# A transformer trunk on one core: the last down projection with the activations as the stationary operand, and a final norm per partition

## The chip, the cores and the metric

The kernel runs on one core of one Trainium2 chip. The metric is the device time of one execution in microseconds (us); a kernel's time is the median of its runs.

## The reference, cut to what matters

A trunk of two layers over 256 tokens of 2048 features, all in fp32. What the change touches is the end of the second layer: the gated MLP, the residual sum and the final norm.

```
def conv_ffn(h, w_up, conv_w, conv_b, w_down):
    up = h @ w_up
    g, val = up[..., :D_FF], up[..., D_FF:]
    g = causal_dwconv(g, conv_w, conv_b)
    return (jax.nn.gelu(g) * val) @ w_down          # D_FF = 5632
...
        h = h + mix
        h = h + conv_ffn(rmsnorm(h, norm_ffn[layer]), ff_w_up[layer], ff_conv_w[layer],
                         ff_conv_b[layer], ff_w_down[layer])
    return rmsnorm(h, norm_final)                   # over the 2048 features of each token
```

## The kernel before

Activations lie feature-major: a tile has 128 features on the partitions and the 256 tokens along the free axis. The residual stream is `h[0..15]`, sixteen such tiles in eight SBUF tensors (lines 307 and 308). A factor of a matmul is held as a pair of float32r parts whose sum is exact: `split` (lines 271 to 280) makes [hi | lo] of an activation, 128x512, in a slot of the pool `s2k` (61 slots), and `convert` (lines 185 to 200) makes `hi` (ScalarE, line 198) and `lo` (VectorE, line 199) of a weight unit. All weights come as one stream of units of 128x1024 (512 KB), loaded by SP (line 175) four ahead and converted two ahead of the unit in use (`next_unit`, lines 202 to 210); `raw` has four buffers, `hi` and `lo` three each.

There are two matmul loops. `wstat` (lines 237 to 248) holds a weight tile stationary: for each 128x128 tile one matmul of hi with the 512 columns [xh | xl] and one of lo with the 256 columns xh. Its output is feature-major, in one of four PSUM buffers `acc`, as two halves that are added afterwards. `astat` (lines 250 to 263) holds the activations stationary: for each k tile and each half t of the tokens three matmuls, xh with hi, xh with lo and xl with hi, over cw weight columns, into one PSUM buffer for each t. Its output has 128 tokens on the partitions. It needs weights in the layout of `mov_stream` (lines 51 to 55) in place of `stat_stream` (lines 37 to 48). It is used with cw of 416 and 512 for z and v of layer 0, and with 512 for the v projection of layer 1 (lines 865 to 871).

Small work is woven into the loops: generators in the list `bg` are advanced a step by `tick()`, which `wstat` calls behind every second k tile and `astat` behind every k and t.

The last stage is `ffn(xs, sq, 1, "nfin", last=True)` at line 967. It makes the 44 tiles `act` (lines 791 to 804) and then calls `residual` (lines 752 to 779): for each of 16 output tiles m a `wstat` of 44 k tiles, two VectorE adds into `h[m]` (lines 770 and 771), a ScalarE product with the norm weight into `nxt` (line 775), and the square of `h[m]` summed on POOL (`Sq.add`, lines 328 to 342), the last one on VectorE. After that comes the final norm (lines 970 to 980): `sq.finish` (lines 354 to 367) sums over the partitions with matmuls against ones, makes the reciprocal root by eleven small VectorE instructions (`rv` at line 360, then `newton`), spreads it over the partitions with four more matmuls and copies it to `R`; then eight tiles are scaled by VectorE and POOL and stored from the queues of SP and ACT.

The instructions of each engine run in the order that the tile framework gives them, mostly that of the program; `pin` keeps an instruction in program order.

Of the kernel before, what the change touches and what calls it, by code (L numbers as in the profile page):

```python
# [36 lines left out]
def stat_stream(w, cols=None, front=0):  # L37
    """[K, N] -> units [U, 128, 1024]: eight 128x128 tiles each, k fastest;
    of the first `front` column tiles the last two k tiles come after the rest."""
    if cols is not None:  # L40
        w = w[:, cols]
    k, n = w.shape
    t = w.reshape(k // P, P, n // P, P).transpose(2, 0, 1, 3)
    if front:
        a = t[:front]
        t = np.concatenate([a[:, :-2].reshape(-1, P, P), a[:, -2:].reshape(-1, P, P), t[front:].reshape(-1, P, P)])
    t = t.reshape(-1, 8, P, P)
    return np.ascontiguousarray(t.transpose(0, 2, 1, 3)).reshape(-1, P, 1024)


def mov_stream(w, cw):
    """[K, N] -> units [U, 128, 2*cw]: two k tiles of a chunk of cw columns each."""
    k, n = w.shape
    t = w.reshape(k // 256, 2, P, n // cw, cw).transpose(3, 0, 2, 1, 4)
    return np.ascontiguousarray(t).reshape(-1, P, 2 * cw)
# [45 lines left out]
@with_exitstack  # L101
def trunk(ctx: ExitStack, tc: tile.TileContext, a, out):
# [17 lines left out]
    def slot(dt=F32):  # L120
        return sp.tile([P, 512], dt, tag="s2k", name=nm("s"))
# [23 lines left out]
    seq = []  # L145

    def add(name):
        ap = a[name]
        for u in range(ap.shape[0]):
            seq.append((ap, u, ap.shape[2]))  # L150
# [16 lines left out]
    def load():  # L167
        """one DMA of weights; the first ones bring the input along."""
        i = st["load"]
        if i >= len(seq):  # L170
            return
        st["load"] += 1
        ap, u, wd = seq[i]
        raw = wp.tile([P, 1024], F32, tag="raw", name=nm("raw"), bufs=4)[:, :wd]
        nc.sync.dma_start(out=raw, in_=ap[u])
        raws.append(raw)
        if i == 0:
            nc.sync.dma_start(out=vec[:, :KD], in_=a["vec"][:, :KD])
        if i < KD // 2:
            nc.sync.dma_start(out=h2[i], in_=a["x0"][i])  # L180
        if i == KD // 2:
            nc.sync.dma_start(out=con, in_=a["con"])
            nc.sync.dma_start(out=vec[:, KD:], in_=a["vec"][:, KD:])

    def convert():
        """weights as a pair of float32r parts whose sum is exact."""
        i = st["conv"]
        if i >= len(seq):
            return
        st["conv"] += 1  # L190
        raw, wd = raws[i], seq[i][2]
        raws[i] = None
        hi = wp.tile([P, 1024], F32R, tag="hi", name=nm("hi"))
        lo = wp.tile([P, 1024], F32R, tag="lo", name=nm("lo"))
        n = 2 if i < 2 else 1
        for c in range(n):
            q = slice(c * wd // n, (c + 1) * wd // n)
            A.copy(out=hi[:, q], in_=raw[:, q])  # L198
            V.tensor_tensor(lo[:, q], raw[:, q], hi[:, q].bitcast(F32), op=ALU.subtract)  # L199
        ready.append((hi, lo))  # L200
# [49 lines left out]
    def astat(kt, xs, cw):  # L250
        pst = [acc(), acc()]
        for k in range(kt):
            if k % 2 == 0:
                hi, lo = next_unit()
            o = (k % 2) * cw
            for t in range(2):
# [14 lines left out]
    def split(src, scale=None, dst=None):  # L271
        """[128,256] fp32 (SBUF or PSUM), times a per-partition scale -> [hi | lo]."""
# [9 lines left out]
    def newton(y, v, t):  # L282
        """y = v ** -0.5"""
# [37 lines left out]
    class Sq:  # L321
        """sum of squares over feature tiles; the last tile goes its own way."""
# [5 lines left out]
        def add(self, src, last=False, join=True):  # L328
# [3 lines left out]
            if last:  # L332
                if join:
                    eng.tensor_tensor(self.acc, self.acc, q, op=ALU.add)
                else:
                    self.parts.append(q)
# [32 lines left out]
        def spread(self, n):  # L369
            """the factor for feature-major tiles alone, on every partition."""  # L370
# [9 lines left out]
    def pending(sq, n=D, wait=6, hold=None):  # L380
        """the RMS factor, made a few steps into the next matmuls."""
# [12 lines left out]
    class Lazy(list):  # L394
        """entries are made when the matmul loop first reaches them."""
# [18 lines left out]
    # small tables that the layers read later  # L414
# [6 lines left out]
    def small_loads():  # L421
        pin(nc.gpsimd.dma_start(out=row, in_=a["row"].partition_broadcast(P)))
        yield
        for i in range(2):
            # spatial weights [j, g, i], block-lower-triangular part
# [38 lines left out]
    # ================= layer 0 mixer =================  # L464
# [6 lines left out]
    def gate_z(pst, c):  # L471
        """silu of a chunk of z; for chunk 0 the first 32 columns are dt."""
# [67 lines left out]
    def conv_tile(b, wname, n, width, taps, bias):  # L540
        """causal depthwise conv of a [128,256] tile along the free axis."""
# [122 lines left out]
    # gMLP, four chunks of 512 channels, the scan's groups woven in  # L664
# [50 lines left out]
    # gating by z, grouped RMS norm, back to feature-major  # L715
# [36 lines left out]
    def residual(kt, xin, wname, last=False, front=0):  # L752
        """front: that many tiles run ahead through all but the last two k tiles."""
# [8 lines left out]
        for m in range(KD):  # L762
# [9 lines left out]
            if last:  # L772
                if m % 2 == 0:
                    nxt.append(slot())
                A.activation(nxt[-1][:, (m % 2) * S:(m % 2 + 1) * S], h[m], AF.Identity, bias=0.0, scale=vc(wname, m))
            else:
                nxt.append(split(h[m], vc(wname, m)))
            sq.add(h[m], m == KD - 1, not last)
# [9 lines left out]
    def ffn(xs, sq, lay, wnext, last=False):  # L788
# [16 lines left out]
        return residual(KF, act, wnext, last)  # L805

    xs, sq = residual(32, Lazy(mix_in), "nf0")
    xs, sq = ffn(xs, sq, 0, "nm1")

    # ================= layer 1 mixer (MLA) =================  # L810
# [19 lines left out]
    def roped(x, o):  # L830
        """rotate the halves of two 64-row heads."""
# [80 lines left out]
    def step(kind, j):  # L912
        """one stage of the attention of heads 2j and 2j + 1."""
# [53 lines left out]
    hw, sq = ffn(xs, sq, 1, "nfin", last=True)  # L967

# [1 line left out]
    _, R, Rp = sq.finish(D)  # L970
    for q in range(KD // 2):
        if q == 0:
            for i in range(2):
                v = hw[q][:, i * S:(i + 1) * S]
                V.tensor_tensor(v, v, Rp, op=ALU.mult)
                (nc.scalar if i else nc.sync).dma_start(out=out[q][:, i * S:(i + 1) * S], in_=v)
            continue
        v = hw[q].rearrange("p (a b) -> p a b", a=2)
        (G if q in (3, 6) else V).tensor_tensor(v, v, R.unsqueeze(1).to_broadcast([P, 2, S]), op=ALU.mult)  # L979
        (nc.scalar if q % 2 else nc.sync).dma_start(out=out[q], in_=hw[q])  # L980
# [74 lines left out]
```

## Time and profile before

| | before |
|---|---|
| median of 3 runs | 2423.49 us |
| lowest and highest run | 2418.5 and 2424.66 us |
| span of the profiled execution | 2419.3 us (the page gives no other time of it) |
| mean granted TensorE clock | 0.995 |
| busy: TensorE, VectorE, ScalarE, POOL | 2386.0, 1582.7, 1189.3, 482.7 us |
| read from HBM, written to HBM | 431.15 MB, 2.10 MB |

A profile shows one execution. Engines are PE (TensorE matmuls), PEld (its weight loads), DVE (VectorE), ACT (ScalarE), POOL (GpSimd) and SP; "q" behind a name is that engine's queue. L133 is line 133, where all matmuls are issued, and L136 that of all transposes, so the names of the tiles tell them apart: `acc` is a projection, `ms` small work. Matmuls are pipelined: the duration of one is longer than the distance from its start to the next one's.

### The profile page before, as it was taken

The numbers are of one execution on the slowest core, as the hardware profiler recorded it, in microseconds if no ns is written. First come the engines' busy times: TensorE is split into PE (matmuls) and PEld (weight loads), VectorE is DVE, ScalarE is ACT, GpSimd is POOL, SyncE is SP. The second block draws the span as 40 slices with busy tenths as digits, with TensorE's granted clock in tenths as the row PEclk, the third lists the DMA queues.
The fourth block names the chain that finished last, engine by engine and source line by source line (L and its number), as shares of the span: only waits on it lengthen the run. The fifth ranks groups of instructions, "written<-read, shape, count | busy, mean of one in ns | idle before, by whom it ended". The sixth has DMA issues, their size and how long they took to land.

```text
span 2419.3 us, 35301 instructions
## 1 busy us (share of the span) xinstructions
PE 2386.0 (99%) x13479; PEld 2072.6 (86%) x13479; DVE 1582.7 (65%) x2371; ACT 1189.3 (49%) x1729; POOL 482.7 (20%) x452
## 2 busy tenths in 40 slices
PE   8999999999999999999999999999999999999997
PEld 6888888988888888888888887788888888888886
DVE  7677777665576666666555577778666666664544
ACT  5654444644455555555444445544555555554442
POOL 4111221022211112111111132123211111111111
PEclk9999999999999999999999999999999999999998
DMA  6565545666666666666666655356666666666664
GB/s 219 166 178 156 160 153 153 188 184 189 184 190 188 189 191 191 191 189 189 191 190 191 190 170 155 96 158 185 196 188 189 190 191 191 188 190 190 191 191 131
DMA packets 121913, 435.54 MB, mean 180 GB/s; under 512 B 13696, under 2 KB 14080, under 8 KB 121744
## 3 DMA queue, kind: packets, MB, share of 16 engines
q1 hardware_dynamic: 120672, 431.02, 59.3%
q8 instruction: 105, 1.72, 0.3%
q0 software_dynamic: 352, 1.10, 0.2%
q10 hardware_dynamic: 720, 1.18, 0.1%
q14 instruction: 64, 0.52, 0.1%
HBM read 431.15 MB, written 2.10 MB: 179 GB/s over the span
## 4 chain that ended last, share of the span: by engine, by line
PE 95%; DVE 2%; issue 1%; POOL 1%; ACT 1%; DMA 0%; SPq 0%; DVEq 0%; POOLq 0%; ACTq 0%
PE acc L133 91%; PE ms L133 4%; DVE lo L199 1%; PE ms L136 1%; DVE s L279 0%; ACT hi L198 0%; DMA raw<-in_z 0%; POOL t L550 0%; DVE t L545 0%; DVE s L979 0%; POOL s L818 0%; DVE s L276 0%; POOL t L331 0%; DVE s L634 0%; DVE t L268 0%
## 5 line engine op out<-in xcount | busy, mean ns | idle before, releaser
L133 PE MATMUL acc<-s,hi 128*128 128x512 f32 x5936 | 2072.9, 394 | 0.0
L133 PE MATMUL acc<-s,lo 128*128 128x256 f32 x5936 | 1656.4, 279 | 3.8 <-DVE lo L199 3.8
L199 DVE TENSOR_TENSOR lo<-raw,hi 128x1024 fp32r<-128x1024 f32 (+2 forms) x824 | 1015.9, 1233 | 700.1 <-ACT hi L198 693.9
L198 ACT CAST hi<-raw 128x1024 fp32r<-128x1024 f32 (+2 forms) x824 | 858.0, 1042 | 1088.3 <-PE acc L133 883.4
L133 PEld LDWEIGHTS acc<-s,hi 128*128 128x128 f32 x5936 | 1112.4, 187 | 255.6 <-issue 3.2
L133 PEld LDWEIGHTS acc<-s,lo 128*128 128x128 f32 x5936 | 1118.8, 188 | 5.6 <-DVE lo L199 4.8
L133 PE MATMUL acc<-hi,s 128*128 128x512 f32 (+1 forms) x640 | 198.6, 385 | 6.2 <-DVE s L279 5.7
L331 POOL TENSOR_TENSOR t<-h 128x256 f32<-128x256 f32 x60 | 66.9, 1114 | 588.1 <-DVE h L771 563.9
L801 POOL TENSOR_TENSOR t<-t,R 128x256 f32<-128x256 f32 x88 | 121.4, 1380 | 313.8 <-ACT t L800 309.9
L798 POOL TENSOR_TENSOR t<-t,R 128x256 f32<-128x256 f32 x88 | 68.9, 783 | 488.7 <-DVE t L268 453.4
L133 PEld LDWEIGHTS acc<-hi,s 128*128 128x128 f32 x640 | 121.4, 192 | 23.7 <-DVE s L279 8.4
L545 DVE SCALAR_TENSOR_TENSOR t<-t,vec,t 128x255 f32<-128x255 f32 (+2 forms) x248 | 120.7, 487 | 14.2 <-ACT t L543 9.7
L133 PE MATMUL acc<-lo,s 128*128 128x416 f32 (+1 forms) x320 | 121.8, 381 | 1.4 <-DVE lo L199 1.4
L268 DVE TENSOR_TENSOR t<-acc,t 128x256 f32<-128x256 f32 x233 | 97.4, 418 | 0.8 <-ACT t L267 0.8
L267 ACT COPY t<-acc 128x256 f32<-128x256 f32 x233 | 83.5, 359 | 0.3 <-PE acc L133 0.3
L133 PE MATMUL ms<-s,s 128*128 128x128 f32 (+4 forms) x424 | 78.2, 307 | 1.1 <-DVE s L930 0.6
L133 PEld LDWEIGHTS ms<-s,s 128*128 128x128 f32 (+1 forms) x424 | 60.1, 189 | 19.9 <-issue 9.0
L342 POOL TENSOR_TENSOR sqacc<-sqacc,t 128x256 f32<-128x256 f32 x60 | 72.8, 1213 | 4.7
L543 ACT ACTIVATE t<-t,vec 128x256 f32<-128x256 f32 x112 | 67.2, 600 | 12.9 <-POOL t L798 7.6
L133 PEld LDWEIGHTS acc<-lo,s 128*128 128x128 f32 x320 | 61.5, 192 | 8.4 <-DVE lo L199 2.1
L279 DVE SCALAR_TENSOR_TENSOR s<-h,vec,s 128x256 fp32r<-128x256 f32 x64 | 56.6, 895 | 1.0 <-ACT s L278 1.0
L803 DVE TENSOR_TENSOR t<-t,t 128x256 f32<-128x256 f32 x88 | 37.4, 426 | 28.6 <-POOL t L801 28.6
(174 smaller groups left out, 811.7 us busy)
## 6 DMA issues: line engine op xcount, KB each, us to landing
raw<-in_up SPq DMA_DIRECT2D x352, 512.0 KB, 4.2
raw<-in_down SPq DMA_DIRECT2D x176, 512.0 KB, 3.6
raw<-in_wout SPq DMA_DIRECT2D x64, 512.0 KB, 3.6
raw<-in_z SPq DMA_DIRECT2D x40, 416.0 KB, 3.6
raw<-in_x SPq DMA_DIRECT2D x32, 512.0 KB, 3.6
raw<-in_v SPq DMA_DIRECT2D x32, 512.0 KB, 3.7
raw<-in_u SPq DMA_DIRECT2D x32, 512.0 KB, 3.9
raw<-in_wo SPq DMA_DIRECT2D x32, 512.0 KB, 3.6
```

Of the source, the lines that this page charges most:

```text
L133: return nc.tensor.matmul(*args, **kw)
L198: A.copy(out=hi[:, q], in_=raw[:, q])
L199: V.tensor_tensor(lo[:, q], raw[:, q], hi[:, q].bitcast(F32), op=ALU.subtract)
L267: A.copy(out=b, in_=ps[:, S:])
L268: V.tensor_tensor(b, ps[:, :S], b, op=ALU.add)
L279: V.scalar_tensor_tensor(x[:, S:], src, scale, x[:, :S].bitcast(F32), op0=ALU.mult, op1=ALU.subtract)
L331: eng.tensor_tensor(q, src, src, op=ALU.mult)
L342: eng.tensor_tensor(self.acc, self.acc, q, op=ALU.add)
L543: A.activation(o, b, AF.Identity, bias=bias, scale=taps[width - 1])
L545: V.scalar_tensor_tensor(o[:, i:], b[:, :S - i], taps[width - 1 - i], o[:, i:], op0=ALU.mult, op1=ALU.add)
L798: G.tensor_tensor(b, b, R, op=ALU.mult)
L801: G.tensor_tensor(o, o, R, op=ALU.mult)
```

## The change

The last down projection goes from `wstat` to `astat`: four chunks of 512 output features, each with 44 k tiles and two halves of the tokens. The weights of that layer are laid out by `mov_stream`. The result has tokens on the partitions, so the residual is needed in that form too: a generator `by_token` transposes the sixteen tiles of `h` on TensorE, four to a PSUM buffer, and copies them to eight slots `ht[t][c]`; it runs in the ticks of the first chunk. It also loads the norm weights, broadcast over the partitions, from POOL's queue. Behind each chunk VectorE adds PSUM to `ht`, ScalarE squares the sum and adds the squares up along the free axis, and POOL multiplies by the norm weight (for half 0 of the last chunk VectorE does it, together with the factor). In the last unit of the last chunk the steps of half 0 come ahead of those of half 1 (`stagger`). The final factor is then one value per partition, made from `ss` by the same eleven small instructions. Eight tiles of 128x512 are scaled by VectorE and ScalarE and stored from the queues of SP, POOL and ACT. The matmuls against ones and those that spread the factor are gone for this norm. The host puts the output together for the new layout.

```
-    def astat(kt, xs, cw):
+    def astat(kt, xs, cw, stagger=False):
         pst = [acc(), acc()]
-        for k in range(kt):
-            if k % 2 == 0:
-                hi, lo = next_unit()
-            o = (k % 2) * cw
-            for t in range(2):
+        for u in range(kt // 2):
+            hi, lo = next_unit()
+            steps = [(k, t) for k in (2 * u, 2 * u + 1) for t in range(2)]
+            if stagger and u == kt // 2 - 1:
+                steps.sort(key=lambda q: q[1])
+            for k, t in steps:
+                o = (k % 2) * cw
                 xh = xs[k][:, t * P:(t + 1) * P]
...
-    hw, sq = ffn(xs, sq, 1, "nfin", last=True)
-
-    # ---- final norm ----
-    _, R, Rp = sq.finish(D)
-    for q in range(KD // 2):
...
+    act = ffn(xs, sq, 1)
+    ht = [[], []]
+    nw = []
+
+    def by_token():
+        for c in range(4):
+            nw.append(slot())
+            pin(nc.gpsimd.dma_start(out=nw[c], in_=a["nfin"][:, c * 512:(c + 1) * 512].partition_broadcast(P)))
+            for t in range(2):
+                ps = pmis()
+                for i in range(4):
+                    tr(ps[:, i * P:(i + 1) * P], h[4 * c + i][:, t * P:(t + 1) * P], ident)
+                yield
+                ht[t].append(slot())
+                A.copy(out=ht[t][c], in_=ps)
+                yield
+
+    bg.append(by_token())
+    ss = tiny([P, 4, 2], "fss", 1)
+    part_sum = tiny([P, 2], "fps", 1)
+    for c in range(4):
+        last = c == 3
+        pst = astat(KF, act, 512, last)
+        if c == 0:
+            flush()
+        for t in range(2):
+            o = ht[t][c]
+            V.tensor_tensor(o, pst[t], o, op=ALU.add)
+            jk = slot()
+            A.activation(jk, o, AF.Square, bias=0.0, scale=1.0, accum_out=ss[:, c, t:t + 1])
+            if not last or t:
+                G.tensor_tensor(o, o, nw[c], op=ALU.mult)
+        if c == 2:
+            V.tensor_tensor(part_sum, ss[:, 0, :], ss[:, 1, :], op=ALU.add)
+            V.tensor_tensor(part_sum, part_sum, ss[:, 2, :], op=ALU.add)
+            V.tensor_scalar(part_sum, part_sum, 1.0 / D, EPS, op0=ALU.mult, op1=ALU.add)
+    v = tiny([P, 2], "rv")
+    V.scalar_tensor_tensor(v, ss[:, 3, :], 1.0 / D, part_sum, op0=ALU.mult, op1=ALU.add)
+    rt = rsqrt(v, [P, 2], "rn")
+    for c in range(4):
+        o = ht[0][c]
+        if c == 3:
+            V.scalar_tensor_tensor(o, o, rt[:, 0:1], nw[c], op0=ALU.mult, op1=ALU.mult)
+        else:
+            V.tensor_scalar(o, o, rt[:, 0:1], None, op0=ALU.mult)
+        nc.sync.dma_start(out=out[c], in_=o)
+        o = ht[1][c]
+        if c == 2:
+            V.tensor_scalar(o, o, rt[:, 1:2], None, op0=ALU.mult)
+        else:
+            A.activation(o, o, AF.Identity, bias=0.0, scale=rt[:, 1:2])
+        (nc.gpsimd if c < 2 else nc.scalar).dma_start(out=out[4 + c], in_=o)
...
-        arrays[f"down{lay}"] = stat_stream(f["ff_w_down"][lay])
+        arrays[f"down{lay}"] = mov_stream(f["ff_w_down"][1], 512) if lay else stat_stream(f["ff_w_down"][0])
```

## Rows read from the trace of the kernel before

**Rows 1.** Busy time of the engines: first the page's line for the whole span, then 240 us of the last down projection by stretch (us, busy us and instructions of each engine, granted TensorE clock, share of the DMA engines, GB/s).

```profile
PE 2386.0 (99%) x13479; PEld 2072.6 (86%) x13479; DVE 1582.7 (65%) x2371; ACT 1189.3 (49%) x1729; POOL 482.7 (20%) x452
...
2160.00:2400.00 240.00, 240.00 (x1387) 211.63 (x1386) 119.44 (x119) 97.50 (x104) 37.03 (x31) 1.00 0.61 182
```

**Rows 2.** The chain of waits in order of time: start us, us, what ran. The first line is its longest piece, the others are from its end.

```profile
670.12 732.16 PE acc L133 x4224
...
2149.95 253.55 PE acc L133 x1463
...
2403.52 0.44 DVE h L770
...
2405.85 0.17 DVE rv L360
...
2407.82 0.17 DVE rny L288
...
2410.45 4.59 DVE s L979 x5
```

**Rows 3.** TensorE in order of time, near the end of the last down projection: start us, us, instruction. Between these two lo matmuls lie 24 pairs.

```profile
2394.88 0.28 PE L133 MATMUL acc<-s,lo 128*128 128x256 f32 x1
...
2403.20 0.28 PE L133 MATMUL acc<-s,lo 128*128 128x256 f32 x1
```

**Rows 4.** The same view in the v projection of layer 1, the loop with stationary activations and 512 columns. Between the first and the last line lie 14 triples, across a chunk end.

```profile
1465.17 0.39 PE L133 MATMUL acc<-lo,s 128*128 128x512 f32 x1
1465.40 0.62 PE L133 MATMUL acc<-hi,s 128*128 128x512 f32 x2
...
1474.69 0.39 PE L133 MATMUL acc<-lo,s 128*128 128x512 f32 x1
```

**Rows 5.** The same view in the z projection, triples of 416 columns, where eight transposes stand (seven in one line, one ahead of them).

```profile
432.92 0.35 PE L133 MATMUL acc<-lo,s 128*128 128x416 f32 x1
...
433.48 0.35 PE L133 MATMUL acc<-lo,s 128*128 128x416 f32 x1
...
433.97 0.94 PE L136 MATMUL ms<-con,s 128*128 128x128 f32 x7
...
434.94 0.35 PE L133 MATMUL acc<-lo,s 128*128 128x416 f32 x1
```

**Rows 6.** Groups of instructions by line and shape, from all engines: count, busy us, mean ns of one, idle time before them.

```profile
L136 PE MATMUL ms<-con,s 128*128 128x128 f32 x80 | 12.8, 274 | 0.1
...
L591 ACT COPY s<-ms 128x512 f32<-128x512 f32 x4 | 2.3, 587 | 1.3 <-PE ms L136 1.3
...
L659 DVE TENSOR_TENSOR s<-ms,s 128x512 f32<-128x512 f32 x8 | 5.1, 685 | 0.7 <-PE ms L133 0.7
...
L722 ACT ACTIVATE s<-s 128x512 f32<-128x512 f32 x8 | 5.0, 628 | 0.0
...
L722 ACT ACTIVATION_READ_ACCUMULATOR s<-s 128x1 f32 x8 | 1.5, 191 | 0.0
...
L726 DVE TENSOR_SCALAR s<-s,gny 128x512 f32<-128x512 f32 x8 | 3.5, 484 | 0.1
...
L617 POOL TENSOR_TENSOR s<-s,w 128x512 f32<-128x512 f32 x4 | 4.2, 1046 | 0.0
...
L661 POOL TENSOR_TENSOR s<-s,s 128x512 f32<-128x512 f32 x4 | 8.8, 2205 | 74.0 <-DVE s L659 74.0
...
L979 POOL TENSOR_TENSOR s<-s,R 128x512 f32<-128x512 f32 x2 | 2.9, 1489 | 17.3 <-ACT R L366 17.3
...
L800 ACT ACT_TABLE_LOAD x2 | 2.6, 1283 | 0.2
```

**Rows 7.** ScalarE and VectorE in order of time in the last down projection: the cast of one weight unit, which waited for TensorE to free its buffer, and the subtraction behind it.

```profile
2167.71 1.05 ACT L198 CAST hi<-raw 128x1024 fp32r<-128x1024 f32 x1 [1.76 <-PE acc L133]
...
2168.79 1.23 DVE L199 TENSOR_TENSOR lo<-raw,hi 128x1024 fp32r<-128x1024 f32 x1 [1.59 <-ACT hi L198]
```

**Rows 8.** VectorE and POOL in order of time in layer 0: small instructions of a reciprocal root (128x4), first without and then with a POOL product beside them.

```profile
388.20 0.17 DVE L286 TENSOR_TENSOR lnt<-lny 128x4 f32<-128x4 f32 x1
...
391.37 0.70 DVE L286 TENSOR_TENSOR lnt<-lny 128x4 f32<-128x4 f32 x1
...
391.20 0.85 POOL L681 TENSOR_TENSOR t<-t,R 128x256 f32<-128x256 f32 x1 [10.01 <-DVE lny L288]
```

**Rows 9.** The stores at the end: the first issue, from the view in order of time; the four that ACT issued at line 980, with min, median and max ns and the first and last start; and three stretches (columns as in rows 1).

```profile
2410.15 0.35 SPq L976 DMA_DIRECT2D out_h<-s  x1
...
L980 ACTq DMA_DIRECT2D out_h<-s x4: 338/358/461, 2411.0 to 2415.1; - x4
...
2412.00:2413.00 1.00, 0.00 (x0) 0.00 (x0) 1.00 (x1) 0.00 (x0) 0.68 (x1) 0.50 1.03 369
...
2416.00:2417.00 1.00, 0.00 (x0) 0.00 (x0) 0.00 (x0) 0.00 (x0) 0.00 (x0) 0.50 1.01 381
2417.00:2418.00 1.00, 0.00 (x0) 0.00 (x0) 0.00 (x0) 0.00 (x0) 0.00 (x0) 0.50 0.14 51
```

**Rows 10.** DMA issues: queue, count, KB each, median us from issue to landing. The first two run in the first 45 us, the third at the end.

```profile
h<-in_x SPq DMA_DIRECT2D x8, 256.0 KB, 5.5
...
s<-in_wsT POOLq DMA_DIRECT2D x2, 256.0 KB, 5.9
...
out_h<-s ACTq DMA_DIRECT2D x4, 256.0 KB, 2.4
```

More of the change, by code (lines that the diff above doesn't have):

```diff
@@ L326, in __init__, with add @@
             self.acc = None
-        def add(self, src, last=False, join=True):
+        def add(self, src, last=False):
             eng = V if last else G
@@ L332, in add @@
             if last:
[L333 to L336, printed above, removed]
+                eng.tensor_tensor(self.acc, self.acc, q, op=ALU.add)
             elif self.acc is None:
@@ L750, in trunk, with residual @@
                 bg.append(finish_group(g))
-    def residual(kt, xin, wname, last=False, front=0):
+    def residual(kt, xin, wname, front=0):
         sq = Sq()
@@ L771, in residual @@
             V.tensor_tensor(h[m], ps[:, S:], h[m], op=ALU.add)
[L772 to L778, printed above, removed]
+            nxt.append(split(h[m], vc(wname, m)))
+            sq.add(h[m], m == KD - 1)
         return nxt, sq
@@ L786, in mix_in, with ffn @@
         return yb[i - 16]
-    def ffn(xs, sq, lay, wnext, last=False):
+    def ffn(xs, sq, lay):
         box = pending(sq)
@@ L804, in ffn @@
             act.append(split(o))
-        return residual(KF, act, wnext, last)
+        return act
     xs, sq = residual(32, Lazy(mix_in), "nf0")
-    xs, sq = ffn(xs, sq, 0, "nm1")
+    xs, sq = residual(KF, ffn(xs, sq, 0), "nm1")
     box = pending(sq)
@@ L966, in trunk @@
     xs, sq = residual(16, ox, "nf1", front=3)
-    hw, sq = ffn(xs, sq, 1, "nfin", last=True)
-    _, R, Rp = sq.finish(D)
-    for q in range(KD // 2):
[L972 to L980, printed above, removed]
+    act = ffn(xs, sq, 1)
@@ L1014 @@
     parts = [("nm0", f["norm_mix"][0]), ("nm1", f["norm_mix"][1]), ("nf0", f["norm_ffn"][0]), ("nf1", f["norm_ffn"][1]),
-             ("nfin", f["norm_final"]), ("cb", f["ev_conv_b"][0]), ("snw", f["ev_ssm_norm_w"][0]),
+             ("cb", f["ev_conv_b"][0]), ("snw", f["ev_ssm_norm_w"][0]),
              ("qn", f["od_q_norm"][0]), ("kvn", f["od_kv_norm"][0]),
@@ L1030 @@
         "bs": np.ascontiguousarray(f["ev_gm_bs"][0].reshape(1, 1024)),
+        "nfin": np.ascontiguousarray(f["norm_final"].reshape(1, D)),
         "z0": zs[:8], "z1": zs[8:],
@@ L1052 @@
     r = run_bass_kernel_spmd(nc, [{"in_" + k: v for k, v in arrays.items()}], core_ids=[0])
-    t = np.asarray(r.results[0]["out_h"]).reshape(8, P, 2, S)
-    return np.ascontiguousarray(t.transpose(3, 0, 2, 1)).reshape(1, S, D)
+    t = np.asarray(r.results[0]["out_h"]).reshape(2, 4, P, 512)
+    return np.ascontiguousarray(t.transpose(0, 2, 1, 3)).reshape(1, S, D)
```

## The prediction

> **What bounds the kernel now.** I read the engines' shares first: TensorE is busy nearly all of the span, and in the last down projection it is busy in every microsecond at the upper clock level of 2.4 GHz (granted 1.00), while VectorE and ScalarE are half free [rows 1]. Then the chain of waits: one unbroken piece of matmuls runs to 2403.5 us, and behind it hangs a tail in which no matmul of weight stands: VectorE adds, the RMS factor, seven scaled tiles, the stores [rows 2]. So the end is set by (a) what TensorE spends on its stream of instructions and (b) that tail: from VectorE's first add at 2403.52 to the end at 2419.3 are 15.78 us. Anything else in the last down projection is covered. The profiled execution's span is 2419.3 us; the page gives no other time for it. It lies 4.2 us under the median of the runs, 2423.49, within their scatter (2418.5 to 2424.66). I make the sum against the span and carry the difference over to the median.
>
> **The stream.** Before, each of 16 x 44 = 704 weight tiles is a pair, 512 and 256 columns: 24 pairs lie between the two rows, 8.32 us, or 0.3467 us a pair [rows 3]; the long piece of the chain gives the same, 732.16 us for 4224 matmuls [rows 2]. After, 4 x 44 x 2 = 352 steps of three matmuls of 512 columns. Lines 250 to 263 run this form already: 14 triples of the v projection of layer 1 take 9.52 us, 0.680 us each [rows 4]. Columns are equal (704 x 768 = 352 x 1536), so at 2.4 GHz a pair has 320 ns of columns and 26.7 beside them, a triple 640 and 40: 13.3 ns per instruction in both, and there are 352 fewer. 704 x 0.3467 = 244.05; 352 x 0.680 = 239.36; **minus 4.69 us**. Weights are used at the same pace (2.77 and 2.72 us per 512 KB unit), so loads stay as they are.
>
> **The transposes.** 32 new PE instructions, in eight groups of four behind the first 16 steps. Where eight transposes stand in a stream of triples, the starts of two neighbouring lo matmuls lie 1.46 us apart instead of 0.56 [rows 5]: 0.90/8 = 0.111 us each, although one lasts 0.272 [rows 6], as they overlap. 32 x 0.111 = **plus 3.56 us**; the bounds are 0.053 (128 columns at 2.4 GHz, worked out from the clock, 1.7 us in all) and 0.272 (8.7 us); I take the row that is the same operation in the same stream. The Trainium skill, "TensorE: Matmul & The Clock Gate", Part 4 (PE-mode transpose), puts one at about 275 ns in a kernel's context; the duration here agrees, the spacing doesn't, and by the page's figure as a cost the 32 would be an estimated 8.8 us and the change a loss on TensorE.
>
> What the transposes need is ready: h was written before the up projection. Their eight ScalarE copies (0.587 each) come at one per two steps, 1.8 us, beside a cast of 1.05 us per unit of four steps, now 3.6 us long; four PSUM buffers stand between. The four broadcast loads of the norm weights sit on POOL's queue, wanted only 60 us later; POOL's products of the last up tile, queued near them, feed act[43], which the new order reads after 58 us (43 x 2 x 0.680) instead of 15. I cost all this at nothing; without that cover a group would wait for a copy, 0.6 us. Removed: 16 times two VectorE adds, a ScalarE product and POOL's squares, all but the last beside matmuls.
>
> **The chunk ends.** New waits stand here three times. VectorE adds (0.685 each) wait for the last matmul, ScalarE's Square (0.63 and 0.19 for its sum) for the add, POOL's product for the Square; queued behind them are the cast (1.05) and the subtraction (1.23) of the weight unit that TensorE wants two units, 5.44 us, later [rows 6, 7]. Counted from the chunk's last matmul: second add done at 0.9, Square 1.6, cast 2.7, the two POOL products (1.05 each) at the latest 3.7, subtraction 4.9. That is 0.5 us inside 5.44, so nothing; the v projection of layer 1, which also evicts 512 columns by both engines at each chunk end, keeps its 0.680 [rows 4]. Upper bound below, as a rival.
>
> **The tail.** Zero is the start of the add behind the last matmul, which lies alike after a stream's end in both. The stagger puts token tile 0 six matmuls ahead, so only tile 1 counts. Add to 0.69; Square and its sum to 1.47; eleven small VectorE instructions (before: 2405.85 to 2407.99, 2.14 us [rows 2]) from 1.50 to 3.64; the first scaled tile 0.485 [rows 6], first store issued at 4.20. Before, that was at 2410.15, or 6.63: gone are the ones-matmuls, the broadcast matmuls, the copy of R.
>
> Against it, POOL's product for tile 1 of the last chunk starts when Square ends, the moment VectorE starts the factor. The trace shows what follows: a 128x4 VectorE product with two SBUF inputs, 0.17 us alone, took 0.70 when a POOL product ran, and both ended together at 392.05 to 392.07 [rows 8]. POOL's 512 columns take 1.05, or 1.49 with VectorE busy beside it [rows 6], so I add **1.0 us**; between 0 (POOL starts later) and 1.4. The Trainium skill, "SBUF — State Buffer", section "Who interferes with whom", says that such an instruction and a POOL instruction that reads SBUF exclude each other for a whole instruction; the row agrees. First store at 5.2.
>
> From first store to end: before 2419.3 - 2410.15 = 9.15 us. 2.10 MB of output flow at 0.37 to 0.38 MB per us [rows 9], so 5.5 us of it is the rate of the transfers, 2.16 is what follows the last byte, and the rest is start-up and the thin first microsecond. After: eight stores of 256 KB on three queues, issued within 3 us, the same rate: 8.55 (no thin start) to 9.15; I take 8.8. The order of scaling (four 0.485 and one 0.69 on VectorE, three on ScalarE) ends by 7.4, before the transfers run dry. End at 5.2 + 8.8 = 14.0 against 15.78: **minus 1.8 us**.
>
> Sum: -4.69 + 3.56 - 1.8 = **-2.9 us**: span 2416.4, median **2420.6**.
>
> **The rivals.**
> *POOL keeps out of the way of the factor* (its start is later, or the small instructions win): the 1.0 us stays saved, -3.9, 2419.6. For it: both wait for the same Square, so either may come first, and only an instruction with two SBUF inputs is known to wait [rows 8].
> *POOL's two stores end last.* For POOL issues the only rows are loads at the start, 5.9 us to landing for 256 KB, beside 5.5 for SP's in the same stretch and 2.4 for ACT's stores at the end [rows 9, 10]. If POOL's descriptors come only when VectorE's scaling ends (7.4), a landing of 5.9 and 1.8 from landing to end give 15.1: -0.7 in the tail, -1.8 in all, 2421.7. The same page's "DVE blocks DMA" box states such a hold; no run here shows it yet.
> *Slower: the chunk ends stall TensorE.* If ScalarE reloads a table at Square (1.283 us [rows 6]) and POOL's product is drawn out by VectorE to 2.2 (the longest 512-column group on POOL [rows 6]), the chain of 4.9 becomes 7.3, 1.9 past 5.44, three times: +5.7, so +2.8, 2426.3. It decides once the chain passes 5.44; against it, Copy and Identity follow Gelu without a load (two loads for 88 Gelus), and 0.5 us is left.
> *The transposes cost their duration*: +5.1, so +2.2, 2425.7. Against it the spacing in rows 5. This is where the page's figure would lead.
> *It doesn't do what it says*: the triples of this stage would have to come slower than in layer 1; at 0.693 (244.05/352) the stream's gain is gone. No row hints at it; it belongs to the unthought.
>
> **How the numbers follow.** Forecast 0.50; POOL out of the way 0.18; POOL stores last 0.12; chunk-end stalls 0.10; transposes at full price 0.04; 0.06 for the unthought, halves on both sides. Range 2416.0 to 2426.5: from the second case less most of the scatter of the runs (they lie up to 5 below their median) to the slower rival. A measurement of this kernel tells 0.3%, 7.3 us, from no change; all cases lie within, so faster 0.06 (half of the unthought, and scatter below the two best cases), within 0.3% 0.90, slower 0.04.
>
> **What would show it.** Triples 0.680 apart in the last 240 us and eight groups of transposes that widen steps by 0.44 each; TensorE without idle time at the three chunk ends; VectorE's first small instructions after the last Square drawn out to about 1.0 us with POOL's product above them; first store 5.2 us after the last add's start, end 14.0. Wrong would be: idle PE behind "lo" near 60, 120 or 180 us into the stage, a table load at Square, or a POOL store landing well after SP's and ACT's.

## The result, and the profile after

The changed kernel takes 2430.49 us (median of 20 runs, 2411.92 to 2436.84), the kernel before 2420.23 beside it (20 runs, 2414.72 to 2425.02): ratio 1.0033, 95% interval 1.0018 to 1.0048. It is 10 us slower where 2.9 us less were forecast. The profiled execution has a span of 2430.0 us and a time of 2431.83.

The chain of waits of the changed kernel, in order of time (start us, us, what), against [rows 2]:

```profile
490.27 179.40 PE acc L133 x1015
670.10 746.24 PE acc L133 x4224
...
1690.47 483.94 PE acc L133 x2791
2174.41 0.44 PE ms L136 x4
...
2187.63 229.21 PE acc L133 x1011
```

The pieces of the kernel before that stand against the first and the third of these:

```profile
490.30 179.39 PE acc L133 x1015
...
1676.17 727.33 PE acc L133 x4196
```

The longest piece is the same work in both kernels: the 4224 matmuls of layer 0's MLP behind the RMS factor. It starts at 670.10 (before 670.12) and lasts 746.24 us instead of 732.16. These 14.08 us are more than the whole loss. The rest of the account, from the same pieces: by the end of that piece the changed kernel is 14.06 us late, by the start of layer 1's MLP 14.30 (1690.47 against 1676.17), at TensorE's last matmul only 13.34 (2416.84 against 2403.50), at the end 10.7 (2430.0 against 2419.3). So the last stage, the only one that the change is about, gained 0.96 us in TensorE's part and 2.64 in the tail: 3.6 us where 2.9 were forecast.

What became slower is seen in a window of 600 us in the middle of that piece. The columns are busy time (count) of PE, PEld, DVE, ACT and POOL, the granted clock, the DMA share and GB/s. First the kernel before, then the changed one:

```profile
700.00:1300.00 600.00, 600.00 (x3463) 524.75 (x3462) 376.14 (x493) 299.09 (x432) 110.59 (x101) 1.00 0.64 190
```

```profile
700.00:1300.00 600.00, 600.00 (x3399) 520.32 (x3398) 368.99 (x486) 294.80 (x429) 103.92 (x99) 1.00 0.60 187
```

TensorE is busy in every microsecond and at the upper clock level (1.00) in both; it simply gets through fewer matmuls, 3399 instead of 3463. Nobody makes it wait: VectorE, ScalarE and the DMA engines all have less to do, as they follow TensorE. The pair of a 512 and a 256 column matmul comes every 353.3 ns instead of 346.7. 2112 pairs by 6.67 ns are 14.08 us. Either pace is a rhythm of its own: in the traces the starts of the pairs lie 350 and 343 ns apart in turn before, and 350, 350 and 360 after.

Both paces occur in both kernels. In the output projection ahead of that piece nearly all pairs come 353.3 ns apart before and after (the piece of 1015 matmuls lasts 179.39 and 179.40 us). Between the two stretches stand the matmuls against ones of the RMS factor. Before, the stream goes on at 346.7 ns behind them; after, at 353.3, and it keeps that for 746 us. In the MLP of layer 1 both kernels run at 346.7.

The tail, in order of time (start us, us, engine, line, operation, buffers, in brackets the idle time before):

```profile
2416.86 0.69 DVE L992 TENSOR_TENSOR s<-acc,s 128x512 f32<-128x512 f32 x1 [0.67 <-PE acc L133]
2417.64 0.63 ACT L994 ACTIVATE s<-s 128x512 f32<-128x512 f32 x1 [0.68 <-issue]
...
2418.39 0.16 DVE L1002 SCALAR_TENSOR_TENSOR rv<-fss,fps 128x2 f32<-128x2 f32 x1 [0.84 <-ACT s L994]
2418.44 1.26 POOL L996 TENSOR_TENSOR s<-s,s 128x512 f32<-128x512 f32 x1 [56.69 <-ACT s L994]
2418.59 1.13 DVE L287 TENSOR_SCALAR rny<-rv 128x2 int32<-128x2 int32 x1
2419.76 0.16 DVE L289 TENSOR_TENSOR rnt<-rny 128x2 f32<-128x2 f32 x1
...
2422.10 2.26 SPq L1010 DMA_DIRECT2D out_h<-s  x4
```

POOL's last product starts 0.05 us behind VectorE's first small instruction; the second small instruction takes 1.13 us instead of the 0.16 of its neighbours and ends with POOL's product. The first store is issued 5.24 us after the add (2416.86).

The transfers at the end: windows with the same columns as above, and the stores of each queue with count, KB and median us to landing.

```profile
2423.00:2424.00 1.00, 0.00 (x0) 0.00 (x0) 1.00 (x2) 0.47 (x1) 0.67 (x2) 0.50 1.02 371
...
2428.00:2429.00 1.00, 0.00 (x0) 0.00 (x0) 0.00 (x0) 0.00 (x0) 0.00 (x0) 0.50 0.58 215
```

```profile
out_h<-s SPq DMA_DIRECT2D x4, 256.0 KB, 2.9
out_h<-s POOLq DMA_DIRECT2D x2, 256.0 KB, 3.8
out_h<-s ACTq DMA_DIRECT2D x2, 256.0 KB, 4.8
```

The flow stands at 371 GB/s from 2423 on and ends 0.58 into the microsecond of 2428, so 1.4 us before the end, where [rows 9] had 0.14 into 2417 and 2.16.

### The profile page after: what moved, and what is told of

Its sections match the earlier page's. It is cut to its first block, busy times and chain, and to the rows that moved or that the text cites. A ratio compares the mean times of both kernels' runs of the same rounds, so it can differ in the third digit from the quotient of the medians.

```text
span 2430.0 us, 34606 instructions
## 1 busy us (share of the span) xinstructions
PE 2399.4 (99%) x13147; PEld 2063.1 (85%) x13147; DVE 1577.8 (65%) x2347; ACT 1192.3 (49%) x1739; POOL 447.0 (18%) x433
## 4 chain that ended last, share of the span: by engine, by line
PE 96%; DVE 2%; issue 1%; ACT 1%; POOL 0%; DMA 0%; SPq 0%; DVEq 0%; POOLq 0%; ACTq 0%
PE acc L133 91%; PE ms L133 4%; PE ms L136 1%; DVE lo L199 1%; DVE s L282 0%; ACT hi L198 0%; POOL t L550 0%; DMA raw<-in_z 0%; DVE t L545 0%; DVE s L279 0%; DVE s L634 0%; POOL t L831 0%; DVE t L271 0%; POOL s L827 0%; DVE s L821 0%
## 5 line engine op out<-in xcount | busy, mean ns | idle before, releaser
L133 PE MATMUL acc<-s,hi 128*128 128x512 f32 x5232 | 1845.1, 398 | 0.0
L133 PE MATMUL acc<-s,lo 128*128 128x256 f32 x5232 | 1463.8, 280 | 3.9 <-DVE lo L199 3.8
L133 PEld LDWEIGHTS acc<-s,hi 128*128 128x128 f32 x5232 | 983.1, 188 | 238.1 <-issue 2.9
L133 PEld LDWEIGHTS acc<-s,lo 128*128 128x128 f32 x5232 | 987.2, 189 | 5.4 <-DVE lo L199 4.9
L133 PE MATMUL acc<-hi,s 128*128 128x512 f32 (+1 forms) x1344 | 419.4, 389 | 5.0 <-DVE s L282 5.0
L133 PEld LDWEIGHTS acc<-hi,s 128*128 128x128 f32 x1344 | 254.9, 191 | 49.1 <-DVE s L282 7.1
L133 PE MATMUL acc<-lo,s 128*128 128x512 f32 (+1 forms) x672 | 259.5, 386 | 1.4 <-DVE lo L199 1.4
L133 PEld LDWEIGHTS acc<-lo,s 128*128 128x128 f32 x672 | 128.3, 191 | 21.9 <-DVE lo L199 2.1
L334 POOL TENSOR_TENSOR t<-h 128x256 f32<-128x256 f32 x45 | 51.3, 1140 | 406.7 <-DVE h L771 393.2
L996 POOL TENSOR_TENSOR s<-s,s 128x512 f32<-128x512 f32 x7 | 10.2, 1470 | 230.9 <-ACT s L994 230.9
```

Source lines behind the costliest of these rows:

```text
L133: return nc.tensor.matmul(*args, **kw)
L334: eng.tensor_tensor(q, src, src, op=ALU.mult)
```

## The experiments

**Which difference turns the pace.** Up to the last stage the two kernels differ in one thing. The final norm weight is no longer in the table of vectors; the table shrinks from 608 to 592 columns, and every buffer allocated behind it (h, the weight buffers, the slots, the small ones) lies 64 bytes per partition lower (by the order of allocation; no trace shows an address). My theory: this shift, not the new last stage, costs the 14 us. The rival: the longer program or the new layout of the weights in HBM does it, or chance.

The changed kernel with 16 columns that nobody reads:

```
-             ("cb", f["ev_conv_b"][0]), ...
+             ("pad", f["norm_final"]), ("cb", f["ev_conv_b"][0]), ...
```

> The changed kernel with sixteen unused columns put back into the vector table, so that every SBUF address and the load of the table are as in the kernel before. Theory A (what moved by those 64 bytes decides which of the two paces the matmul pairs of layer 0's MLP take): its long piece falls back to 732 us (346.7 ns a pair) in nearly all runs, and the time is 2413 to 2418, about 4 us under before. Theory B (the pace is a matter of chance or of the time of arrival, not of addresses): runs fall on both sides, near 2415 and near 2430, in some mix. Theory C (something else of the change, such as the longer program, sets it): near 2430 as the changed kernel.

Median 2415.11 (12 runs), ratio 0.9982 (0.9970 to 0.9993). In its chain of waits:

```profile
673.22 732.16 PE acc L133 x4224
```

The kernel before with the 16 columns taken out (the last norm takes the weight of another norm: the same work, other values):

```
-    hw, sq = ffn(xs, sq, 1, "nfin", last=True)
+    hw, sq = ffn(xs, sq, 1, "nf1", last=True)
...
-             ("nfin", f["norm_final"]), ("cb", f["ev_conv_b"][0]), ...
+             ("cb", f["ev_conv_b"][0]), ...
```

> The kernel before with the sixteen columns of the final norm weight taken out of the vector table (the last layer is scaled by the weight of another norm instead, same work), so that SBUF addresses and the load of the table are as in the changed kernel, and nothing else. Theory A: the slow pace comes to layer 0's MLP here too, 746 us for its piece, 2434 in most runs. Theory B: a mix of 2420 and 2434. Theory C: 2420 as before.

Median 2433.35 (6 runs), ratio 1.0050 (1.0030 to 1.0071); its chain of waits:

```profile
670.02 746.24 PE acc L133 x4224
```

So the loss comes without any of the new last stage, and leaves with the 16 columns while the new stage stays. The longer program and the layout in HBM fall as causes, and chance alone with them: five of these six runs are at 2433 or above (one at 2419.46), and of the twelve with the columns back the longest is 2423.85. The changed kernel once more, unaltered, beside these:

> The changed kernel unchanged, for the share of its runs in each pace on this chip. All theories: some 80% near 2430, some 20% near 2414; a profile of the fast kind would show 732 us for layer 0's MLP and the same last stage of 256.4 us.

Median 2428.69 (12 runs; one of them took 4848.78 us, has no trace and is left out of the ratio), ratio 1.0030 (1.0014 to 1.0046), and the piece lasts 746.24 us again.

**The load or the place.** The table is also one transfer, and a smaller one. The changed kernel with a wider buffer and the load as it was, by 64 bytes:

```
-            nc.sync.dma_start(out=vec[:, KD:], in_=a["vec"][:, KD:])
+            nc.sync.dma_start(out=vec[:, KD:a["vec"].shape[1]], in_=a["vec"][:, KD:])
...
-    vec = cp.tile([P, a["vec"].shape[1]], F32, name="vec")
+    vec = cp.tile([P, a["vec"].shape[1] + 16], F32, name="vec")
```

> The changed kernel with 64 bytes per partition left unused behind the vector table: every buffer behind it lies where it lay before the change, but the load of the table stays 592 columns. If the place of the buffers decides the pace of layer 0's MLP, its pairs come 346.7 ns apart, the profile has a piece of 4224 matmuls of about 732 us, and the median is about 2415, as in the run with the 16 columns back. If the load's size or arrival decides, the piece is 746 us and the median about 2429.

Median 2417.29 (12 runs), ratio 0.9989 (0.9979 to 0.9999), and in the chain of waits:

```profile
668.70 732.16 PE acc L133 x4224
```

The place decides, not the transfer. With 128 bytes in the same line (+ 32 instead of + 16):

> The same with 128 bytes left unused, so that the buffers lie 64 bytes behind their place before the change, and at the same remainder of 128 as in the changed kernel. If the remainder of 128 decides: pairs 353.3 ns apart, median about 2429. If any other place than that of the changed kernel will do (or only the exact place of before matters, by some other order of events): 346.7 ns and about 2415, or either by chance.

Median 2443.03 (4 runs), ratio 1.0095 (1.0081 to 1.0109). Its chain of waits:

```profile
668.97 746.25 PE acc L133 x4224
...
1690.97 493.24 PE acc L133 x2791
```

Layer 0's MLP runs as in the changed kernel, which shares the remainder of 128; but here the MLP of layer 1 is slow as well (493.24 us instead of 483.94), which it never was at that remainder before. Its slow stretch starts earlier: layer 1's attention projection ahead of it lasts 83.38 us for 472 matmuls (353.3 ns a pair) instead of 81.82. A rule of the remainder alone doesn't describe it.

**Whose place.** 64 unused bytes behind h and the tables, so that only the weight buffers, the slots and the small buffers go back to their place of before:

```
     cst = cp.tile([64, S], F32R, name="cst")
+    cp.tile([P, 16], F32, name="pad")
```

> The changed kernel with 64 bytes per partition left unused behind the kernel's long-lived buffers: h, the vector table and the rotary tables lie as in the changed kernel, the weight buffers, the slots and the small buffers lie where they lay before the change. If the place of these decides the pace of layer 0's MLP: 346.7 ns a pair, a piece of 4224 matmuls of about 732 us, median about 2416. If the place of h decides: 353.3 ns, 746 us, about 2429.

Median 2417.06 (10 runs), ratio 0.9989 (0.9976 to 1.0001), piece 732.16 us: h doesn't have to go back. Then for the small buffers alone, with the sum of squares that the ones-matmuls read:

```
     ident, ones = C("ident"), C("ones")
+    tiny([P, 16], "pad", 1)
```

> The changed kernel with 64 bytes left unused ahead of the last pool alone, that of the small buffers: only these (among them the sum of squares, which the ones-matmuls read where the pace is decided) lie where they lay before the change, weights and activations as in the changed kernel. If the operand of the ones-matmuls decides: 732 us for the piece of 4224, about 2416. If the weights' or the activations' place decides: 746 us, about 2429.

Median 2427.26 (10 runs), ratio 1.0021 (1.0003 to 1.0040), piece 746.24 us. Four of the ten runs lie at 2412 to 2421 and the others at 2426 or above, so the small buffers alone don't bring the fast pace back in most runs. Then for the slots and the small buffers, but not the weights (`sp.tile([P, 16], F32, tag="pad", name="pad", bufs=1)` at the same line):

> The changed kernel with 64 bytes left unused between the weight buffers and the slots: h and the weight buffers lie as in the changed kernel, the slots with the activations and all small buffers lie where they lay before the change. If the activations' place decides the pace of layer 0's MLP: 346.7 ns a pair, a piece of about 732 us, median about 2417. If the weight buffers' place decides: 353.3 ns, 746 us, median about 2429.

Median 2437.98 (4 runs), ratio 1.0071 (1.0056 to 1.0086). Neither expectation holds: the chain of waits has paces that no other run had.

```profile
670.82 736.86 PE acc L133 x4224
1687.42 487.05 PE acc L133 x2791
2187.75 235.91 PE acc L133 x1011
```

736.86 us for 2112 pairs are 348.9 ns a pair, no mixture of the other two (the starts lie 349, 347 and 351 ns apart in turn), and the triples of the last stage come 0.700 us apart (235.91/337) instead of 0.680. In this run alone the distance between the weight buffers and the slots differs from that of before, by 64 bytes. So in this layout the place of the stationary operand relative to the moving one has a price of its own, unless another buffer that moved along with the slots has it; which of the two decides between 346.7 and 353.3 when both move together stays open.

**What the pace hangs on in time.** If the pace is chosen anew at each interruption of the stream and then kept, small matmuls put into it must turn it, with all buffers where the changed kernel has them. `nudge(n)` issues n matmuls of ones with the unit matrix into a spare PSUM buffer:

```
+            if lay == 0 and j > 1:
+                nudge(1 + j % 4)
             psg = wstat(KD, xs)
```

> The changed kernel with 1 to 4 small 128-column matmuls, of no use, ahead of each of 42 up tiles of layer 0's MLP. If an interruption of the stream decides the pace anew, the pace of the pairs changes at some of the 42 places and holds between them; cost of the small matmuls some 105 x 0.11 = 12 us, with some 7 us back if half of the stretches become fast: 2435. If once slow stays slow, 2442; if any interruption restores the fast pace, 2428, and the profile shows 346.7 ns from the first one on.

Median 2445.25 (5 runs), ratio 1.0098 (1.0085 to 1.0111), more than each of the three times expected: a matmul of a nudge costs 0.22 us, not 0.11. From the chain of waits ("ms" is the nudge; a matmul of it shows as two instructions):

```profile
710.87 0.22 PE ms L133 x2
711.09 11.30 PE acc L133 x64
722.40 0.44 PE ms L133 x4
722.84 11.10 PE acc L133 x64
```

All 42 stretches keep to this: 11.30 us for 32 pairs (353.1 ns) behind one or three nudges, 11.10 (346.9) behind two or four; the last, longer one runs at 346.7 behind four. But the up tiles alternate between PSUM buffers in the same rhythm. So the count and the tile's parity were taken apart, with 23 nudges in layer 0's MLP and four in the output projection:

```
+    COUNT = {2: 2, 4: 1, 6: 2, 7: 1, 9: 2, 10: 2, 11: 2, 13: 1, 14: 1, 16: 4, 17: 3, ...}
...
+            if lay == 0 and j in COUNT:
+                nudge(COUNT[j])
```

> The changed kernel with one to four small matmuls put in ahead of 23 of the 44 up tiles of layer 0 and of four of the output projection's column tiles, in an order in which the count and the tile's parity don't go together (2 at tile 2, 1 at 4, 2 at 6, 1 at 7, and so on). If an odd count gives 353.3 ns and an even one 346.7, the pace follows the count; if the parity of the tile decides (even 353.3), the PSUM buffer that follows does; if it changes over at each interruption whatever the count, it strictly alternates; else no rule of these. One look: time about 2430 to 2438.

2427.03 us in its one run. From its chain of waits:

```profile
682.39 0.44 PE ms L133 x4
682.84 22.20 PE acc L133 x128
705.03 0.22 PE ms L133 x2
705.25 22.62 PE acc L133 x128
...
762.26 0.44 PE ms L133 x4
762.71 11.10 PE acc L133 x64
773.81 0.44 PE ms L133 x4
774.25 11.10 PE acc L133 x64
```

22.20 us for 64 pairs are 346.9 ns, 22.62 are 353.4. All 27 stretches follow the count: an even number of nudges gives the fast pace, an odd one the slow, whatever the tile's parity and whatever the pace ahead (two even ones in a row give fast and fast). The output projection, slow to its end in every run so far, turns fast behind two.

One nudge of four in the whole kernel (`if lay == 0 and j == 3: nudge(4)`):

> The changed kernel with four small matmuls ahead of the fourth up tile of layer 0, and nothing else moved: all buffers lie as in the changed kernel. If the pace is decided anew at each interruption and then kept, the pairs are 353.3 ns apart for the first three tiles and 346.7 from there on to the end of the down projection: 2112 pairs less 96, 13.4 us back for 0.4 us spent, median about 2416. If the place of the buffers sets the pace by itself, it stays at 353.3 and the median is about 2429.

Median 2418.43 (11 runs), ratio 0.9994 (0.9985 to 1.0002), 2 us over what was expected. In the chain of waits the four nudges stand at 698.69; the piece ahead of them runs at 353.3 ns a pair, the one behind them, 4060 matmuls to the end of the down projection, at 346.7:

```profile
669.72 28.97 PE acc L133 x164
698.69 0.89 PE ms L133 x8
...
699.58 703.74 PE acc L133 x4060
```

One interruption of 0.89 us gives 13.5 us back (2030 pairs by 6.67 ns), 12.6 net: the three pieces add up to 733.60 instead of 746.24. No buffer was moved for it.

**A version that uses it.** The changed kernel with two nudges ahead of the second column tile of the output projection and two ahead of the second up tile of layer 0, and with POOL's last product given to VectorE:

```
+                if kt == 32 and m == 1:
+                    nudge(2)
...
+            if lay == 0 and j == 1:
+                nudge(2)
...
-            if not last or t:
+            if not last:
                 G.tensor_tensor(o, o, nw[c], op=ALU.mult)
...
-        if c == 2:
+        if c == 3:
+            V.scalar_tensor_tensor(o, o, rt[:, 1:2], nw[c], op0=ALU.mult, op1=ALU.mult)
+        elif c == 2:
```

> The changed kernel with two small matmuls ahead of the second column tile of layer 0's output projection and two ahead of the second up tile of its MLP, and with the last product with the norm weights taken from POOL: VectorE scales that tile in one instruction, as it does for token tile 0. If an even count brings the pace of 346.7 ns wherever it stands: 2064 and 480 pairs at 6.67 ns less, 13.8 and 3.2 us, for about 0.46 us each; the small instructions of the factor are no longer held, 1.0 us of the tail. In all 17 us under the changed kernel, median about 2412.5, 0.997 of the kernel before. If the pace hangs on more than the count: 2416 (one stretch stays at 353.3) to 2429. If POOL's hold was hidden by the transfers anyway, the tail stays at 13.1 us and all is 1 us later.

Median 2416.28 (12 runs), ratio 0.9991 (0.9980 to 1.0001). The MLP is fast (725.93 us for 4188 matmuls, 346.7 ns a pair). The tail, in order of time:

```profile
2401.91 0.69 DVE L1001 TENSOR_TENSOR s<-acc,s 128x512 f32<-128x512 f32 x1 [0.67 <-PE acc L133]
...
2403.64 0.17 DVE L287 TENSOR_SCALAR rny<-rv 128x2 int32<-128x2 int32 x1
...
2406.19 2.26 SPq L1019 DMA_DIRECT2D out_h<-s  x4
```

The same instruction that took 1.13 us takes 0.17 without POOL's product beside it; the first store is issued at 4.28 and the kernel ends 12.09 us after the add (2414.0), 1.05 earlier than 13.14. POOL's hold was worth what it showed. The output projection, however, stayed slow (175.02 us for 990 matmuls). TensorE in order of time there, the nudges and the first matmul behind them:

```profile
492.69 0.61 PE L133 MATMUL ms<-con 128*128 128x128 f32 x4
493.15 0.50 PE L133 MATMUL acc<-s,hi 128*128 128x512 f32 x1
```

The kernel before with the same two nudges in the output projection does the same:

> The kernel before, with only the two small matmuls ahead of the second column tile of layer 0's output projection. By the theory of the count its pairs come 346.7 ns apart instead of 353.3: 480 x 6.67 = 3.2 us less, 0.46 spent, so 2.7 us under the kernel before, ratio 0.9989, and MLP and all else as before. If the interruption is passed on, the MLP's pace may change with it: 14 us more, about 2432.

Median 2419.88 (12 runs), ratio 1.0004 (0.9993 to 1.0015); 175.02 us for 990 matmuls, and the MLP 732.16 as before. So the count doesn't hold at that tile, in either kernel.

The traces show why. The first matmul behind the nudges waits for VectorE's split of the last activation tile (0.48 us from 492.62 on). The same wait stands in the changed kernel without nudges:

```profile
494.32 0.48 DVE L282 SCALAR_TENSOR_TENSOR s<-ms,vec,s 128x256 fp32r<-128x256 f32 x1
494.40 0.39 PE L133 MATMUL acc<-s,hi 128*128 128x512 f32 x1
...
494.85 0.50 PE L133 MATMUL acc<-s,hi 128*128 128x512 f32 x1
```

The thirteen pairs ahead of it, from 490.23 to 494.40, come 347 ns apart; behind it the pace is 353.3 to the end of the projection, in the kernel before as well. So the pace changes at a wait of TensorE too, and nudges ahead of it don't prevent that. Put ahead of the third column tile (`m == 2`) in both:

> As the version with both pairs of small matmuls, but the pair of the output projection stands ahead of its third column tile instead of the second, where the stream waited 0.1 us behind the pair and kept 353.3 ns. By the theory of the count, with no wait behind the interruption: 448 pairs at 6.67 ns less, 3.0 us, for 0.46 spent, so 2.5 us under that version, median about 2413.8, ratio to the kernel before about 0.9977. If the second interruption in the output projection is also passed over: as that version, 2416.3, 0.9991.

Median 2413.61 (8 runs), ratio 0.9975 (0.9965 to 0.9985), span 2410.2. TensorE in order of time at the nudges, then the chain of waits:

```profile
503.75 0.60 PE L133 MATMUL ms<-con 128*128 128x128 f32 x4
504.12 0.47 PE L133 MATMUL acc<-s,hi 128*128 128x512 f32 x1
```

```profile
503.92 0.45 PE ms L133 x4
504.36 160.17 PE acc L133 x924
```

> The kernel before, with only the two small matmuls ahead of the third column tile of layer 0's output projection. By the theory of the count 448 x 6.67 = 3.0 us less for 0.46 spent: 2.5 us under the kernel before, ratio 0.999; layer 0's MLP and all else as before. If the pace is kept as it was behind the pair ahead of the second tile: 0.5 us over the kernel before, 1.0002.

Median 2418.15 (11 runs), ratio 0.9990 (0.9981 to 0.9999); 160.16 us for the 924 matmuls, 346.7 ns a pair. At the third tile the next matmul starts 0.37 us after the first nudge, at the second it started 0.46 after it: the 0.09 us are that wait. Taken together, the changed kernel with nudges and the shorter tail is 4.5 us under the kernel before with the nudge, 6.1 under the kernel before as it was.

**What the 64 bytes changed.** Read together, the profiles say it more closely than the theory above. The ones-matmuls of the RMS factor are an interruption of two instructions. Where the weight buffers and slots lie as before, the stream behind them is fast, whether it was slow ahead of them (five profiles, the kernel before among them) or fast (the run just above). Where these lie 64 bytes lower, the stream goes on as it came: slow in seven profiles, but fast in the two in which nudges had made the output projection fast. One of these two is the run with 23 and four nudged places:

```profile
626.48 38.14 PE acc L133 x220
664.62 0.43 PE ms L133 x2
665.05 17.34 PE acc L133 x100
```

38.14 us for 110 pairs and 17.34 for 50 are 346.7 and 346.8 ns. So in these profiles the shift did not by itself make the matmuls slow: it took away a turn to the fast pace, and the stream had been slow since the wait at 494.85.

## Why the prediction was wrong, point by point

- **The step that failed** is one that stands in no line of the sum: "I make the sum against the span" with terms for the last stage alone sets all the rest of the kernel at zero. The diff's change to the vector table was not costed. It moves every later buffer by 64 bytes, and with it the pace of layer 0's MLP behind the RMS factor stayed slow, where it had turned fast: +14.08 us. Shown: the same 64 bytes cost it in the kernel before, and giving them back by any of three edits (16 unread columns, an unloaded strip, a strip behind h) brings 732.16 us back. None of the rivals held this; it belongs to the "unthought", and is five times the forecast gain.
- **The stream and the transposes** were right: 229.21 us for 337 triples are 0.680 each; eight groups of four transposes last 0.44, 0.110 a transpose (forecast 0.111), so that rival falls. TensorE's part gained 0.96 us (forecast 4.69 - 3.56 = 1.13; 0.90/8 is 0.1125 and not 0.111, and [rows 6] have 274 ns and not 0.272, which changes no sum by more than 0.1). The Trainium skill, "TensorE: Matmul & The Clock Gate", Part 4, puts a PE-mode transpose at about 275 ns; the trace agrees with it as a duration (274 ns, [rows 6]) and not as a cost in a stream (110 ns).
- **The chunk ends** cost nothing, as forecast: the chain has TensorE alone from 2187.63 to 2416.84, over all three of them.
- **The tail**: POOL's hold of the small instructions was right in kind and size (first store at 5.24, forecast 5.2; 1.05 us came back when POOL was taken out, 0.96 of them in the instruction that was held). The instruction held is not of the kind that [rows 8] had shown, one with two SBUF inputs: it has a single input. The Trainium skill, "SBUF — State Buffer", section "Who interferes with whom", counts `tensor_scalar` among the operations that can enter a mode with two ports, if their operands meet its conditions, and then shut out POOL or are shut out by it; the 1.13 us beside POOL against 0.17 without it agree, though no run shows the mode. The term that was mis-sized is first store to end: 7.9 us instead of 8.8, as the flow was full within 0.9 us of the first issue and its last byte left only 1.4 us to the end instead of 2.16. The tail gained 2.64, not 1.8.
- **POOL's two stores** didn't end last: 3.8 us to landing against 4.8 for ACT's.
- With the weight buffers and slots back at their place the change measures 0.9982, 0.9989 and 0.9989 of the kernel before, so 4.4, 2.7 and 2.7 us less, against the 2.9 forecast. The intervals of the three reach from 7 us less to no change, so this agrees with the forecast and doesn't prove its size; the pieces of the profile (3.6) are the closer measure.

What stays open: why 64 bytes decide what happens at that one interruption, and not at others; and by what the matmuls are served faster in one rhythm than in the other. The profiled executions show the pace of one run each; that 4 of the changed kernel's 20 runs lie at 2411.9 to 2415.8 and the others at 2428.99 or above, with 2414.42 and 2430.35 at the same mean granted clock of 0.994, suggests that the turn is not the same in every run, but no trace of such a run was taken. An execution's span also varies by some us with its mean granted clock (the kernel before, beside the experiments: 2425.56 at 0.992 and 2413.62 at 0.995), so pieces of the chain were compared above and not spans.

## What to carry to other kernels

A change is costed by what it moves too: read the allocation and the tables in the diff, and compare the long pieces of stages that were not touched before looking at the stage that was. A stream of matmuls at the upper clock level had more than one pace here: divide a piece's time by its pairs, in both kernels and in each stretch, and where it is the slower one, try a short interruption with another count of instructions, or a strip of unused bytes, before rewriting anything. Keep POOL's products off the moment at which VectorE makes the factor that everyone waits for.

## What the runs showed of the hardware that was not expected

Pairs of a 512 and a 256 column matmul, with a weight load each, come 346.7 or 353.3 ns apart at the same granted clock of 1.00, and a stretch keeps its pace, over up to 4224 matmuls, until something stands between: other matmuls, or a wait (346.7 ahead of that at 494.85, 353.3 behind it). Nudges set it by their count, four or eight instructions fast and two or six slow, in all 42 + 27 places of two runs, both with the buffers of the changed kernel. A shift of all buffers by 64 bytes decided whether the ones-matmuls of one norm turned a slow stream fast. A shift of the slots and small buffers against the weight buffers by 64 bytes gave 348.9 ns a pair and made triples 0.700 us instead of 0.680.
